# Rotary embedding and score matrices: which five loads GpSimd issues, and where their leftover rows go

## The chip, the core and the metric

The kernel runs on one core of a Trainium2 chip. The core has a matrix engine (TensorE, PE in the profile), three engines for elementwise work (VectorE or DVE, ScalarE or ACT, GpSimd or POOL), a queue engine (SyncE or SP) and sixteen DMA engines that move data between HBM and the on-chip memory SBUF. The metric is the device time of one execution in microseconds (us); lower is better.

## The reference: what is computed

For 16 batches, 512 positions, 16 heads and 64 dimensions, q and k are rotated by tables of cosines and sines, and then, for each position, every head of q is multiplied with the heads of k at all positions of the same batch and head:

```python
q1, q2 = q[..., :half_dim], q[..., half_dim:]
q_rot = np.concatenate([
    q1 * cos_q - q2 * sin_q,
    q1 * sin_q + q2 * cos_q
], axis=-1)
# k_rot in the same way
scores = np.einsum('bshd,bthd->bsht', q_rot, k_rot)
```

All is float32. The inputs q and k are 33.6 MB each, the output (16, 512, 16, 512) is 268.4 MB, so the kernel writes four times what it reads.

## The kernel before, in words

A batch is cut into four tiles of 128 positions (position p*4+c goes to partition p of tile c), so there are 64 tiles in all. Per tile, VectorE rotates q and k in place with three instructions of 128x1024 each (`rope`: two products, lines 153 and 154, and one sum, line 158). PE transposes the rotated rows against an identity matrix, four 128x128 blocks into a PSUM bank (`transposed`, line 174), and VectorE (q) or ScalarE (k, from batch 2 on) copies a bank to SBUF (line 189). PE then computes the scores of one tile, two heads at a time, in eight steps (`scores`, line 205), ScalarE copies each 128x1024 result into a staging buffer (line 212), and after the eighth step the buffer, 4 MB, is stored (line 192). There are three staging buffers.

The first batch is handled in small pieces: its q and k come in several early loads, and its output leaves in sixteen stores of 1 MB (line 215). From batch 1 on, a tile's turn in the main loop contains the eight score steps, the transposes of the next tile of q (at steps 1 and 3) and of the tile of k four ahead (steps 5 and 6), and the rotation of q two tiles ahead and of k five tiles ahead. The order of instructions on every engine is the written order.

The inputs of batches 1 to 15 are loaded whole: `load(which, b)` reads 2 MB, 128 rows of 16 KB. There are two buffers for q and two for k. In the main loop, `load("q", b+2)` stands behind the third tile of batch b and `load("k", b+3)` behind the fourth. Most loads are one DMA on SP's queue (line 126), the same queue that carries all stores. Such a DMA is cut over the sixteen DMA engines, eight rows for each. Stores are cut in the same way (eight rows of 32 KB for each engine).

Five loads go another way, through `load_around`. GpSimd issues them on its own DMA queue, q0 in the profile, where a DMA of n rows with n up to 15 takes n engines one after the other, starting at a cursor that stands behind the last engine used. The main part of the load is the first 120 rows: they go to fifteen engines, eight rows each, in two pieces of 8 KB per row. The cursor is placed so that these fifteen are all but engine 4 (`SLOW = 4`: the DMA starts at engine 5). The cursor is placed by tiny DMAs (`move_cursor`, line 87): n rows of a few bytes into a scratch tile move it by n. The remaining eight rows, 120 to 127, are the leftover. For the loads of k, GpSimd issues them as eight pieces of 2 KB per row with the cursor at 8, one row per engine on engines 8 to 15. For the loads of q, ScalarE's DMA queue (q10) issues them, eight rows on the eight lowest engines, 0 to 7, engine 4 among them. All of these pieces are issued on line 102.

The names that matter below: `RELIEVED` says which loads go this way and in which order (the value counts them, and the first one, 0, resets the cursor); `pieces(queue, lo, hi, F)` issues rows lo to hi in parts of F elements.

Of the kernel before, what the change touches and what calls it, by code (L numbers as in the profile page):

```python
# [10 lines left out]
def kernel(  # L11
# [8 lines left out]
    nc = tc.nc  # L20
# [4 lines left out]
    B, S, H, D = q.shape  # L25
    HD = D // 2
    P = 128
    C = S // P
# [45 lines left out]
    batches = {}  # L74

    RELIEVED = {("q", 6): 0, ("k", 7): 1, ("q", 11): 2, ("k", 12): 3, ("q", 15): 4}
    SLOW = 4
    scratch = const_pool.tile([P, 96], fp32, name="scratch")
    tiny = [0]  # L80

    def move_cursor(n):

        y = tiny[0]
        tiny[0] += 1
        src = bass.AP(q.tensor, 512 * y, [(512, n), (64, 2), (1, 2)])
        nc.gpsimd.dma_start(scratch[:n, 4 * y : 4 * y + 4].rearrange("p (a b) -> p a b", a=2), src)

    def load_around(which, b, t):

        n, E, SMALL = 120, C * H * D, C * H * D // 8
        x = RELIEVED[which, b]
        d = dram[which][b]

        def pieces(queue, lo, hi, F):
            k = E // F
            src = bass.AP(d.tensor, d.offset + lo * E + E - F, [(E, hi - lo), (-F, k), (1, F)])
            v = t[lo:hi].rearrange("p c e -> p (c e)")  # L100
            dst = bass.AP(v.tensor, v.offset + E - F, [v.ap[0], (-F, k), (1, F)])
            queue.dma_start(dst, src)  # L102

        if x == 0:
            nc.gpsimd.inc_swdge_sem([], [], mode="reset_dge_cursor")
        else:

            move_cursor(16 - SLOW)
        if x % 2:
            move_cursor(8)  # L110
            pieces(nc.gpsimd, n, P, SMALL)
        move_cursor(SLOW + 1)
        pieces(nc.gpsimd, 0, n, E // 2)
        if not x % 2:
            pieces(nc.scalar, n, P, SMALL)

    def load(which, b):

        if b >= B:
            return  # L120
        t = in_pool.tile([P, C, H * D], fp32, tag=which + "_in", name=which + "_sb")
        batches[which, b] = t
        if (which, b) in RELIEVED:
            load_around(which, b, t)
        else:
            nc.sync.dma_start(t.rearrange("p c (h d) -> p c h d", h=H), dram[which][b])
# [199 lines left out]
```

## Time and profile before

| what | us |
|---|---|
| median of three runs | 792.46 (792.38 to 793.31) |
| the profiled execution, its span from the first to the last instruction | 789.9 |
| PE busy | 687.7 (87%) |
| ACT busy | 561.2 (71%) |
| DVE busy | 543.8 (69%) |
| POOL busy | 11.9 (2%) |

The profile gives the profiled execution's time as its span; the 2.5 us between it and the median lie outside of the span (start and end of a launch). The page's slices cut the span into 40 equal parts; the digit of the DMA row is the mean busy share of the sixteen DMA engines in tenths, 9 standing for 90% or more. DMA queues are listed with packets, megabytes and their share of the time of sixteen engines: q1 is SP's queue, q0 GpSimd's, q10 ScalarE's, and q8 and q14 fetch instructions. A row of waits reads: who waited, for whom, microseconds in total, how many times, and the longest. A row of DMA issues gives the tile, the queue, how often, the size of each and the median time from issue to landing.

The HBM traffic is 67.24 MB read and 268.44 MB written, 425 GB/s over the span.

### The profile page before, as it was taken

How to read it: one execution, taken by the hardware profiler on the slowest of the kernel's cores; microseconds unless marked ns; L12 is line 12 of the kernel's file. 1: busy time of each engine (PE TensorE's matmuls, PEld its weight loads, DVE VectorE, ACT ScalarE, POOL GpSimd, SP SyncE). 2: the span in 40 equal slices, each digit the busy share in tenths (PEclk: the TensorE clock that was granted, in tenths of full speed). 3: DMA queues.
4: the chain of work that ended last, by engine and by line, in shares of the span. 5: the costliest groups of instructions: out<-in, count | busy, mean ns of one | idle time of the engine just before them, and what ended most of it. 6: DMA issues, size and time to landing. Idle time of an engine off the chain costs nothing.

```text
span 789.9 us, 7753 instructions
## 1 busy us (share of the span) xinstructions
PE 687.7 (87%) x3072; PEld 297.4 (38%) x3072; DVE 543.8 (69%) x516; ACT 561.2 (71%) x647; POOL 11.9 (2%) x24
## 2 busy tenths in 40 slices
PE   4999998989978989798897988989899798899960
PEld 2444443433423434243343433434334343344420
DVE  7999987667855859566676666767678486587400
ACT  3888886866847868486685865877577586588770
POOL 0000000000001000000000000100000000000000
PEclk9999999999998999899899898999899899899995
DMA  9999999999999999999999999999999999999997
GB/s 353 421 426 440 429 431 435 424 434 440 428 427 429 429 425 406 428 431 436 430 431 434 427 431 427 429 432 429 427 437 422 437 433 433 428 431 436 430 431 339
DMA packets 19100, 336.18 MB, mean 426 GB/s; under 512 B 2376, under 2 KB 3656, under 8 KB 4936
## 3 DMA queue, kind: packets, MB, share of 16 engines
q1 hardware_dynamic: 16288, 324.61, 96.1%
q0 software_dynamic: 1872, 10.10, 3.1%
q10 hardware_dynamic: 904, 0.98, 0.4%
q8 instruction: 24, 0.39, 0.2%
q14 instruction: 12, 0.10, 0.0%
HBM read 67.24 MB, written 268.44 MB: 425 GB/s over the span
## 4 chain that ended last, share of the span: by engine, by line
DMA 46%; PE 39%; DVE 7%; ACT 4%; issue 1%; ACTq 0%
DMA out_dram<-st 45%; PE ps L205 29%; PE bank L174 9%; ACT st L212 4%; DVE part L153 2%; DVE early L154 1%; DVE early L158 1%; DMA early<-in_q_dram 1%; DVE k_sb L158 1%; DVE k_sb L154 1%; DVE kT_t L189 0%; DVE q_sb L154 0%; DVE q_sb L158 0%; ACTq L321 0%; DVE qT_t L189 0%
## 5 line engine op out<-in xcount | busy, mean ns | idle before, releaser
L212 ACT COPY st<-ps 128x1024 f32<-128x1024 f32 x512 | 495.0, 1020 | 193.7 <-DMA out_dram<-st 109.1
L205 PE MATMUL ps<-kT_t,qT_t 64*128 64x512 f32 x2048 | 545.6, 650 | 64.3 <-ACT st L212 64.1
L205 PEld LDWEIGHTS ps<-kT_t,qT_t 64*128 64x128 f32 x2048 | 183.3, 196 | 255.3 <-issue 135.4
L189 DVE COPY qT_t<-bank 128x512 f32<-128x512 f32 x118 | 81.5, 690 | 186.5 <-PE bank L174 186.5
L174 PEld LDWEIGHTS bank<-ident,q_sb 128*128 128x128 f32 x480 | 55.4, 151 | 100.5 <-issue 97.6
L174 PE MATMUL bank<-ident,q_sb 128*128 128x128 f32 x480 | 86.8, 308 | 0.4 <-PE ps L205 0.4
L174 PEld LDWEIGHTS bank<-ident,k_sb 128*128 128x128 f32 x480 | 50.3, 140 | 94.6 <-issue 42.3
L174 PE MATMUL bank<-ident,k_sb 128*128 128x128 f32 x480 | 78.6, 287 | 1.2 <-DVE qT_t L189 1.2
L153 DVE TENSOR_TENSOR part<-k_sb,ss_t 128x1024 f32<-128x1024 f32 x60 | 72.9, 1215 | 9.3 <-DMA k_sb<-in_k_dram 9.2
L189 ACT COPY kT_t<-bank 128x512 f32<-128x512 f32 x122 | 72.4, 598 | 6.9 <-PE bank L174 6.9
L154 DVE TENSOR_TENSOR k_sb<-k_sb,cos_t 128x1024 f32<-128x1024 f32 x60 | 73.5, 1225 | 2.0
L158 DVE TENSOR_TENSOR k_sb<-k_sb,part 128x1024 f32<-128x1024 f32 x60 | 73.5, 1225 | 2.1
L154 DVE TENSOR_TENSOR q_sb<-q_sb,cos_t 128x1024 f32<-128x1024 f32 x60 | 73.5, 1225 | 2.1
L153 DVE TENSOR_TENSOR part<-q_sb,ss_t 128x1024 f32<-128x1024 f32 x60 | 73.5, 1224 | 2.0
L158 DVE TENSOR_TENSOR q_sb<-q_sb,part 128x1024 f32<-128x1024 f32 x60 | 72.9, 1215 | 0.0
L174 PE MATMUL bank<-ident,early 128*128 128x128 f32 x64 | 10.5, 316 | 12.2 <-DVE early L158 9.7
L174 PEld LDWEIGHTS bank<-ident,early 128*128 128x128 f32 x64 | 8.3, 161 | 17.3 <-issue 13.9
L153 DVE TENSOR_TENSOR part<-early,ss_t 128x1024 f32<-128x1024 f32 x8 | 9.8, 1222 | 5.7 <-DMA early<-in_k_dram 4.9
L102 POOL DMA_DIRECT2D q_sb<-in_q_dram x3 | 2.3, 754 | 617.4 <-PE bank L174 617.4
L158 DVE TENSOR_TENSOR early<-early,part 128x512 f32<-128x512 f32 x16 | 10.3, 685 | 0.2
L154 DVE TENSOR_TENSOR early<-early,cos_t 128x1024 f32<-128x1024 f32 x8 | 9.8, 1225 | 0.3
L189 ACT COPY qT_t<-bank 128x512 f32<-128x512 f32 x10 | 5.7, 628 | 3.3 <-PE bank L174 3.3
(12 smaller groups left out, 15.9 us busy)
## 6 DMA issues: line engine op xcount, KB each, us to landing
out_dram<-st SPq DMA_DIRECT2D x60, 4096.0 KB, 25.2
k_sb<-in_k_dram SPq DMA_DIRECT2D x13, 2048.0 KB, 27.7
q_sb<-in_q_dram SPq DMA_DIRECT2D x12, 2048.0 KB, 27.6
out_dram<-st SPq DMA_DIRECT2D x16, 1024.0 KB, 14.5
q_sb<-in_q_dram POOLq DMA_DIRECT2D x3, 1920.0 KB, 29.2
k_sb<-in_k_dram POOLq DMA_DIRECT2D x2, 1920.0 KB, 43.2
early<-in_k_dram SPq DMA_DIRECT2D x1, 1536.0 KB
early<-in_q_dram SPq DMA_DIRECT2D x1, 1536.0 KB, 12.4
```

What stands on the lines that cost most here:

```text
L102: queue.dma_start(dst, src)
L153: nc.vector.tensor_tensor(pv, xs, ss, op=mult)
L154: nc.vector.tensor_tensor(xc, xc, cs, op=mult)
L158: nc.vector.tensor_tensor(y, y, z, op=add)
L174: nc.tensor.transpose(bank[:, x, :], src, ident)
L189: copy(out=dst, in_=src)
L205: nc.tensor.matmul(out=po, lhsT=lhs[64 * r : 64 * r + 64, :], rhs=rh, start=True, stop=True)
L212: nc.scalar.copy(out=so, in_=si)
```

## The change

The five loads that GpSimd issues are now all of q: batches 5, 8, 11, 13 and 15. Before, they were q of batch 6, k of 7, q of 11, k of 12 and q of 15. The main part is the same: rows 0 to 119 on all engines but 4.

The leftover rows now go to four engines, 14, 15, 0 and 1 (`AHEAD = 14`: the first of the four), always on GpSimd's queue: the cursor is moved to 14, rows 120 to 123 are issued (one row per engine, two parts of 8 KB), the cursor is moved by 12 and so is back at 14, rows 124 to 127 are issued in the same way, the cursor is moved by 3 to engine 5, and then come the 120 rows. So each of the four engines moves two leftover rows per load, 32 KB, and ScalarE issues no part of a load any more. In the first of the five the cursor starts from a reset (move by 14), in the others from engine 4, where the 120 rows leave it (move by 10).

```diff
-    RELIEVED = {("q", 6): 0, ("k", 7): 1, ("q", 11): 2, ("k", 12): 3, ("q", 15): 4}
-    SLOW = 4
+    RELIEVED = {("q", 5): 0, ("q", 8): 1, ("q", 11): 2, ("q", 13): 3, ("q", 15): 4}
+    SLOW, AHEAD = 4, 14
...
-        n, E, SMALL = 120, C * H * D, C * H * D // 8
+        n, E = 120, C * H * D
...
         if x == 0:
             nc.gpsimd.inc_swdge_sem([], [], mode="reset_dge_cursor")
-        else:
-
-            move_cursor(16 - SLOW)
-        if x % 2:
-            move_cursor(8)
-            pieces(nc.gpsimd, n, P, SMALL)
-        move_cursor(SLOW + 1)
+        move_cursor(AHEAD if x == 0 else (AHEAD - SLOW) % 16)
+        pieces(nc.gpsimd, n, n + 4, E // 2)
+        move_cursor(12)
+        pieces(nc.gpsimd, n + 4, P, E // 2)
+        move_cursor((SLOW + 1 - AHEAD - 4) % 16)
         pieces(nc.gpsimd, 0, n, E // 2)
-        if not x % 2:
-            pieces(nc.scalar, n, P, SMALL)
```

## The prediction

> **What bounds the kernel now.** I read the page's slices first, then its chain, then the queues, then the transfers in narrow windows at the end of the span.
>
> ```profile
> span 789.9 us, 7753 instructions
> DMA  9999999999999999999999999999999999999997
> DMA 46%; PE 39%; DVE 7%; ACT 4%; issue 1%; ACTq 0%
> q1 hardware_dynamic: 16288, 324.61, 96.1%
> q0 software_dynamic: 1872, 10.10, 3.1%
> q10 hardware_dynamic: 904, 0.98, 0.4%
> q8 instruction: 24, 0.39, 0.2%
> q14 instruction: 12, 0.10, 0.0%
> ```
>
> The DMA engines are full in every slice but the last, and the five queues add up to 99.8% of sixteen engines. The chain names PE for 39%, but PE waits there for stage buffers, and so for stores. The bytes do not change here, so a gain can come only from how they are spread over the sixteen engines. The last microseconds show how uneven they are now (windows 781 to 783.5, to 786.5, to 787.5 and to 790 us; each engine's last packet is the 4-byte semaphore write of the last store, so "under 512 B" counts the engines that finish):
>
> ```profile
> DMA packets 33, 0.95 MB, mean 380 GB/s; under 512 B 4, under 2 KB 4, under 8 KB 4
> ...
> DMA packets 30, 0.88 MB, mean 295 GB/s; under 512 B 3, under 2 KB 3, under 8 KB 3
> ...
> DMA packets 9, 0.16 MB, mean 164 GB/s; under 512 B 4, under 2 KB 4, under 8 KB 4
> ...
> DMA packets 5, 0.00 MB, mean 0 GB/s; under 512 B 5, under 2 KB 5, under 8 KB 5
> ```
>
> Four engines are done 5 to 6 us before the last five. To say which, I followed the packet records from end to start: on one engine a packet starts 3 to 4 ns before the recorded end of the one before it, and the order of sizes on each queue is known, so the records fall into sixteen chains from 15 us on, with no idle gap over 0.5 us. The trace names no engine; the split loads do. Eight chains move the small k pieces that GpSimd issues (engines 8 to 15 by the cursor), eight the small q pieces of ScalarE's queue (0 to 7), and one of these eight never gets a data packet of the 120-row loads (4). Ends of the last store:
>
> - upper eight: 782.35, 782.53, 786.35, 786.67, 787.87, 788.25, 788.55, 788.62
> - lower eight: 783.22, 783.32, 785.43, 785.89, 787.05, 787.32, 787.34, 788.52; engine 4 is 787.34 or 788.52, since its chain can't be told from another's for a while
>
> The mean is 786.2. The 24 fetches of q8 (16 KB, 0.88 to 1.05 us each, and the store packet beside one some 0.4 us longer) go round eight chains: the six late upper ones and two lower ones, three each. Those of q14 fall on lower chains. The four early chains carry no fetch. Engine 4 is slow in another way: its 32 KB store packets take about 1246 ns in most stages against 1213 on the others, and 1500 beside a 120-row load.
>
> **The change, part by part.** Durations are those of the profiled execution. Its span is 789.9; the median of the runs is 792.46, so I add 2.5 for what lies outside the span.
>
> *Leftover rows onto four engines.* In each of five loads eight 16 KB rows go to engines 14, 15, 0 and 1: two rows, four 8 KB packets each. 20 packets at 309 ns (every 8 KB packet of q0 on nearly every chain) are 6.18 us per receiver; the worst chain mean, 315 ns, would make 6.3. I take 6.18.
>
> *Old leftover pieces gone.* An upper engine loses eight 4 KB packets (26.23 of q0 time less 25.04 on a chain without them: 1.19 us). A lower one loses 24 pieces of 2 KB and their semaphores on q10: 2.04 us. ScalarE loses three DMA issues (0.72 to 1.29 us); it is 71% busy and ends no wait here, so nothing. If that cover failed it would be under 3 us spread over three stages.
>
> *Engine 4.* It keeps five skipped loads and loses its 2.04 us of q pieces. Its excess over 1213 ns near the two relieved pairs and the last load is about 6, 5 and 0.6 us by the chains; alone the q loads cost 0.6 to 2 each, the k loads 3.3 to 4.3. Five q loads make 3 to 10 instead of some 11.5. Between "one microsecond more" and "eight less" I take 2 to 6 less: it ends well before the others and decides nothing.
>
> *Cursor moves and empty turns.* 30 DMAs on q0 instead of 18: twelve more semaphore packets, four more cursor moves, and on engines that get no piece two placeholders per piece (before, four per k piece on the lower eight). About 35 tiny packets at 7 to 9 ns are 0.3 us per engine. Upper bound: the 290 ns that a turn costs engine 4 beside a 120-row load, 20 turns, 5.8 us; lower bound nothing. I take 0.3, since the lower engines' empty turns at 262 to 267 us are followed by 1213 ns store packets as usual.
>
> *GpSimd's queue and the landing of q.* All five loads now have two pieces and two cursor moves ahead of the 120 rows.
>
> ```profile
> DVE part L153 <- DMA k_sb<-in_k_dram: 9.2, 2, 4.6
> POOL q_sb L102 <- PE bank L174: 617.4, 3, 225.4
> q_sb<-in_q_dram POOLq DMA_DIRECT2D x3, 1920.0 KB, 29.2
> k_sb<-in_k_dram POOLq DMA_DIRECT2D x2, 1920.0 KB, 43.2
> ACT st L212 <- DMA out_dram<-st: 109.1, 41, 6.2
> ```
>
> A q load with nothing ahead lands in 29.2 us, a k load behind pieces in 43.2, and VectorE waited 4.6 us for each such k. On an engine q0 and q1 take turns, one packet each, so what stands ahead costs turns: 2+1, 1+1, 2+1, 1+1, ten turns at 1.22 us, and four more issues on GpSimd, 2.3 us. So q lands 42 to 44 us after the first issue (with a k load of SP's queue in between, whose packets take 0.61 us, some 4 us less). It is needed, by the first product on it, 40.9, 41.3 and 41.3 us after GpSimd's issue for batches 6, 11 and 15. So VectorE waits 0 to 3 us at up to five places. Behind it stand the qT copy of the next tile, then PE's transposes into that bank, four groups later. The cover is the stores already queued: mid-kernel each is issued 6 to 15 us before the fastest engine is done with the one before; the least is 3.2 us (issue at 731.09, first landing of the previous store 734.31). The k waits of 4.6 left no gap in any chain, so these cost nothing; without the cover it is at most 3 us, and only the last load, at 709, comes where stages are as short as 10.02 us. The k waits go, and were hidden too. SP loses the q loads of batches 5, 8, 13 and gets k 7, k 12 and q 6; GpSimd starts a q load some 6.5 us before SP would (227.75 against a store at 234.23), which moves no byte off an engine.
>
> *Sum, by engine:*
> - receivers, upper: 782.5 + 6.18 - 1.19 + 0.3 = 787.8; lower: 783.3 + 6.18 - 2.04 + 0.3 = 787.7
> - upper six with fetches: 788.62 - 1.19 + 0.3 = 787.7 at the latest
> - other lower ones: 788.52 - 2.04 + 0.3 = 786.8 at the latest
>
> The last end moves from 788.6 to 787.8: 0.8 us earlier, a span of 789.1, a time of 791.7 (-0.1%).
>
> **Rivals.**
>
> *Better balance* (0.25). Perfect balance would end all at the mean, 786.2 and 0.3 more: 2.1 us less, 790.4. What could bring it there: at 299 to 308 us, just behind the first pair, load packets on all chains take up to 1765 ns instead of 611, about 1 us per engine, and again weakly at 545 to 553. If the pairs cause that, it goes: 0.8 + 1.0, 790.7. Against it: nothing in the records ties the two.
>
> *A receiver is not an early engine* (0.12, the other side). The trace shows that two upper and two lower engines are early, not that they are 14, 15, 0 and 1. For it speaks that the fetches run through two lower and six upper chains in a fixed cycle, which fits 6 to 13 in a row; a falling order would fit too and make 8 and 9 the early ones. Then a late upper engine gets the rows: 788.6 + 6.18 - 1.19 + 0.3 = 793.9, 5.3 us more, 797.7. It costs over 0.2% as soon as one receiver ends after 784.9 now. Against a slow engine 15: no upper chain has a mean store packet above 1217 ns. The Trainium skill (DMA: Bandwidth & Descriptors, Latency and other measured facts) says that engines 7 and 15 are usually slower in traces, which would speak against giving 15 more; the trace disagrees, its slow engine is among the lower eight and skips the 120-row loads, so I give that rule no more than a part of this chance. By it the sum would be near this rival's, by the trace it stays as above.
>
> *Late q in the last stages* (0.06). If batch 15 lands like the k rows, waiting 4.6 us and 2.3 for the issues, less the 3.2 of margin: 3.7 us lost of the gain, 795.4. It decides from a wait of 3.2 us on.
>
> *The cursor misses* (0.03). Moves of 14, 10, 4 and 3 rows are not in this trace (5, 8, 12 and 120 are). If one did not advance by one engine per row, engine 4 would get five loads back, 80 packets of 309 ns: some 24 us more, about 815.
>
> **Numbers.** Forecast, with nearby outcomes inside 0.2%: 0.54. That 0.2% (1.6 us) is about what a measurement of this kernel can tell from no change. Faster 0.25 is the first rival; slower 0.21 is the other three. The range reaches from perfect balance (790.3) to a loss of 1.2 us (793.7: tiny packets at a quarter of their upper bound, or a late batch 15); it leaves out the wrong receivers, the cursor and the worst of the late q, some 0.18. The likeliest case's own range is 790.9 to 792.6.
>
> **What would show it.** Last store: engines finishing from about 784 to 787.8, none between 781 and 783.5. Queue q0 up by 0.1 to 0.2 points of its share and q10 down by 0.1. VectorE waiting for q_sb up to 3 us, k_sb waits gone, slices still full. It is wrong if four engines finish several us after the rest, if DMA slices fall below 9, or if engine 4's store packets stay above 1500 ns for long.

## The result, and the profile after

The changed kernel takes 797.12 us (796.24 to 797.77) against 792.88 for the kernel before beside it: 1.0051 times as long, 95% interval 1.0040 to 1.0063, 4.2 us slower. The forecast was 791.7. The profiled execution has a span of 795.4 and a time of 797.33, so 1.9 us lie outside the span. (It is 1.8 to 2.0 in the executions of both kernels measured since; the prediction's 2.5 was this and a profiled execution before that was some 0.6 to 0.7 faster than its median.)

The page of the changed kernel: span, slices, the chain, and the queues with packets, megabytes and share.

```profile
span 795.4 us, 7765 instructions
DMA  9999999999999999999999999999999999999996
DMA 49%; PE 37%; DVE 5%; ACT 5%; issue 1%; ACTq 0%; DVEq 0%
q1 hardware_dynamic: 16288, 324.61, 95.5%
q0 software_dynamic: 2320, 10.49, 3.4%
q10 hardware_dynamic: 688, 0.59, 0.2%
q8 instruction: 24, 0.39, 0.2%
q14 instruction: 13, 0.10, 0.0%
```

The slices are still full and the bytes of the queues are what the change says (0.39 MB moved from q10 to q0), yet the span is 5.5 longer. Nothing waits for a late q or k: among the waits that a DMA ends, those of VectorE are for the first batch alone, and ScalarE's for a free staging buffer is what it was (109.1 before). The 120 rows land 37.8 us after their issue (last line).

```profile
ACT st L208 <- DMA out_dram<-st: 110.6, 36, 6.7
...
DVE part L149 <- DMA early<-in_k_dram: 4.9, 1, 4.9
...
q_sb<-in_q_dram POOLq DMA_DIRECT2D x5, 1920.0 KB, 37.8
```

So the loss must lie in how the sixteen engines end. These are the windows 785 to 790, to 792, to 793.5 and to 796 of the changed kernel; "under 512 B" counts engines that finish.

```profile
DMA packets 46, 1.08 MB, mean 216 GB/s; under 512 B 13, under 2 KB 13, under 8 KB 13
...
DMA packets 5, 0.10 MB, mean 49 GB/s; under 512 B 2, under 2 KB 2, under 8 KB 2
...
DMA packets 1, 0.03 MB, mean 22 GB/s; under 512 B 0, under 2 KB 0, under 8 KB 0
...
DMA packets 1, 0.00 MB, mean 0 GB/s; under 512 B 1, under 2 KB 1, under 8 KB 1
```

From 792 on one engine works alone, for two more microseconds. The packet records, followed into sixteen chains as before, say which: the receivers are the four chains with 100 packets of 8 KB on q0. They end at 793.97, 791.48, 790.68 and 788.32; the other twelve at 786.2 to 789.4. The last receiver carries three fetches of q8 (16 KB each), the second six of q14; the other two carry none. So two of the four receivers are not early engines.

The mean over the sixteen chains rose as well, from 786.2 to 788.5. By class, for one engine: 8 KB packets and leftovers 24.9 us before, 26.5 after; SP's load packets 0.3 more; tiny packets 0.25 more. The 8 KB packets take 310 to 470 ns instead of 309 on most of the twelve others near the loads of batches 13 and 15, where the store queue almost ran empty: a store is issued at 595.76, and the first landing of the previous one is at 595.86. On one chain it did run empty, four times between 695 and 737 us, for 0.2 to 0.9 us each. The margin was 3.2 us at the least before. It went as the landings of one store spread over 12 us (6 to 8.5 before): a staging buffer comes free only when the slowest engine is done with it. Why an 8 KB packet then takes longer is not shown.

### The profile page after: what moved, and what is told of

It reads as the page before. It is cut to its first block, busy times and chain, and to the rows that moved or that the text cites. A ratio compares the mean times of both kernels' runs of the same rounds, so it can differ in the third digit from the quotient of the medians.

```text
span 795.4 us, 7765 instructions
## 1 busy us (share of the span) xinstructions
PE 684.2 (86%) x3072; PEld 295.2 (37%) x3072; DVE 544.5 (68%) x516; ACT 561.7 (71%) x647; POOL 19.0 (2%) x36
## 4 chain that ended last, share of the span: by engine, by line
DMA 49%; PE 37%; DVE 5%; ACT 5%; issue 1%; ACTq 0%; DVEq 0%
DMA out_dram<-st 48%; PE ps L201 28%; PE bank L170 9%; ACT st L208 5%; DVE part L149 2%; DVE early L154 1%; DVE k_sb L150 1%; DVE k_sb L154 1%; DVE early L150 1%; DVE kT_t L185 0%; DMA early<-in_k_dram 0%; DVE q_sb L150 0%; DVE q_sb L154 0%; ACTq L317 0%; DVE qT_t L185 0%
## 5 line engine op out<-in xcount | busy, mean ns | idle before, releaser
L201 PE MATMUL ps<-kT_t,qT_t 64*128 64x512 f32 x2048 | 543.8, 648 | 73.3 <-ACT st L208 73.1
L170 PE MATMUL bank<-ident,q_sb 128*128 128x128 f32 x480 | 85.0, 303 | 0.9 <-PE ps L201 0.9
L102 POOL DMA_DIRECT2D q_sb<-in_q_dram x15 | 9.8, 652 | 653.0 <-PE bank L170 509.1
L87 POOL DMA_DIRECT2D scratch<-in_q_dram x15 | 8.7, 581 | 0.4 <-issue 0.4
## 6 DMA issues: line engine op xcount, KB each, us to landing
q_sb<-in_q_dram POOLq DMA_DIRECT2D x5, 1920.0 KB, 37.8
```

Of the source, the lines that this page charges most:

```text
L170: nc.tensor.transpose(bank[:, x, :], src, ident)
L201: nc.tensor.matmul(out=po, lhsT=lhs[64 * r : 64 * r + 64, :], rhs=rh, start=True, stop=True)
```

## The experiments

Two theories at first. R: the loss is placement, two rows per load on engines that are not early. S: it is what every engine pays (the other loads, ten more turns ahead of the 120 rows, more cursor moves, later q). All times are medians, beside the kernel before on the same chip; ratios have 95% intervals.

| run | time | ratio | interval |
|---|---|---|---|
| the change | 797.12 | 1.0051 | 1.0040 to 1.0063 |
| new loads, old leftovers | 792.56 | 1.0003 | 0.9994 to 1.0012 |
| old loads, new leftovers | 798.41 | 1.0073 | 1.0057 to 1.0090 |
| receivers 15, 0, 1, 2 | 795.24 | 1.0035 | 1.0022 to 1.0048 |
| receivers 11, 12, 13, 14 | 797.04 | 1.0057 | 1.0043 to 1.0072 |
| receivers 15, 0, 7, 8 | 806.26 | 1.0176 | 1.0159 to 1.0193 |
| eight receivers, two pieces (30 DMAs) | 795.19 | 1.0033 | 1.0020 to 1.0046 |
| the same, 8 more moves (38) | 795.13 | 1.0037 | 1.0023 to 1.0050 |
| eight receivers, one piece (20 DMAs) | 793.09 | 1.0000 | 0.9992 to 1.0009 |
| the same, piece cut in two (25) | 793.91 | 1.0017 | 1.0007 to 1.0026 |
| one piece, 10 more moves (30) | 793.53 | 1.0013 | 1.0005 to 1.0022 |
| before, scratch 32 columns wider | 795.29 | 1.0041 | 1.0028 to 1.0053 |
| before, scratch 128 columns wider | 792.77 | 1.0002 | 0.9993 to 1.0011 |

Four more runs are given in the text: the two with markers, and two with more moves in a wider scratch tile.

### The two halves of the change

The new choice of loads with the old way for the leftover rows:

```diff
-    RELIEVED = {("q", 6): 0, ("k", 7): 1, ("q", 11): 2, ("k", 12): 3, ("q", 15): 4}
+    RELIEVED = {("q", 5): 0, ("q", 8): 1, ("q", 11): 2, ("q", 13): 3, ("q", 15): 4}
```

> One part of the change alone: the five loads are q of batches 5, 8, 11, 13 and 15, but the leftover rows go where they went before (ScalarE's queue for three loads, GpSimd on engines 8 to 15 for two). Theory R (two of the four receivers were not early engines; the last engine is a receiver that also carries fetches of q8): no receiver is overloaded, so 791.5 to 793.5, within 0.2% of before, and the last engine ends 5 us earlier than in the changed kernel. Rival S (the choice of loads costs: five q loads, late ones above all, let the queue of stores run dry on the fast engines): 795 to 798, most of the loss stays.

And the other half, the changed kernel with the loads of before:

```diff
-    RELIEVED = {("q", 5): 0, ("q", 8): 1, ("q", 11): 2, ("q", 13): 3, ("q", 15): 4}
+    RELIEVED = {("q", 6): 0, ("k", 7): 1, ("q", 11): 2, ("k", 12): 3, ("q", 15): 4}
```

> The other part alone: the loads of before (q 6, k 7, q 11, k 12, q 15), but the leftover rows on engines 14, 15, 0 and 1. R: the same 160 KB on the same four engines, so 796 to 798, some 0.5% slower than before, one engine 2 us or more behind all others in the last store. S: 792 to 794, at most a third of the loss, since the pairs and not five q loads set the pace of the stores.

The first took 792.56, no change; the second 798.41. So the choice of loads costs nothing, and the leftover rows carry the whole loss. Windows 785 to 790, to 793, to 794.5 and to 797 of the second show the same two stragglers (one of the 14 is the last packet of the store before, at 785.84):

```profile
DMA packets 49, 1.15 MB, mean 229 GB/s; under 512 B 14, under 2 KB 14, under 8 KB 14
...
DMA packets 6, 0.16 MB, mean 55 GB/s; under 512 B 1, under 2 KB 1, under 8 KB 1
...
DMA packets 2, 0.03 MB, mean 22 GB/s; under 512 B 1, under 2 KB 1, under 8 KB 1
DMA packets 1, 0.00 MB, mean 0 GB/s; under 512 B 1, under 2 KB 1, under 8 KB 1
```

By the chains they are again the receiver with three q8 fetches (795.2) and the one with six q14 (793.5). The second half is 1.3 us slower than the whole change (the intervals overlap); in it a k load with pieces ahead comes late, and VectorE waits for it:

```profile
DVE part L149 <- DMA k_sb<-in_k_dram: 36.6, 3, 19.8
```

### Which engines carry the fetches

Marker DMAs with packets of sizes that nothing else has, so that a chain shows its engine. First sixteen of two rows in the changed kernel, then fifteen of three rows in the kernel before, behind each of two loads (each moves the cursor by 3, so each engine gets two or three of the sizes). The small tile that takes the markers is not shown:

```diff
+    def mark(first):
+        for j in range(first, first + 8):
+            w = 20 + j
+            src = bass.AP(q.tensor, 4096 * j, [(512, 2), (1, w)])
+            nc.gpsimd.dma_start(marks[2 * j : 2 * j + 2, :w], src)
...
+        if x == 0:
+            mark(0)
+            move_cursor(3)
+            mark(8)
```

> The changed kernel with sixteen tiny DMAs of two rows each, of sixteen different sizes, behind the first split load: each lands on two neighbouring engines by the cursor, so that a chain of packets can be named by the two sizes that it holds. It costs some 34 tiny packets, 0.3 us per engine, and 797 to 798. R: of engines 14, 15, 0 and 1 one of the first two carries three fetches of q8 and ends last, one of the last two carries six of q14, and two carry none; two early engines are among 2 to 13. S: the names do not matter; the last engine need not be a receiver.

```diff
+        if x in (0, 2):
+            for j in range(15):
+                w = 10 + j
+                src = bass.AP(q.tensor, 4096 * j, [(512, 3), (64, 2), (1, w)])
+                nc.gpsimd.dma_start(marks[3 * j : 3 * j + 3, : 2 * w].rearrange("p (a b) -> p a b", a=2), src)
```

> The kernel before with fifteen tiny DMAs of three rows each (two runs of a size of its own per row) behind the split loads of q 6 and of q 11. Each takes three neighbouring engines and moves the cursor by three, three times round the sixteen with another offset each time, so that the three sizes on a chain of packets give its engine. Some 60 tiny packets, 0.5 us per engine: 792 to 795. R: the eight chains that fetch for q8 include just one of the engines 14 and 15; of 0 and 1 one carries the six fetches of q14; the early engines are one of 14 and 15, one of 0 and 1, and at least two others between 2 and 13. If 14, 15, 0 and 1 turn out to be the four early ones, R falls.

The first told little: all sixteen markers fell on the same two chains, both of them receivers, so a plain two-row DMA did not follow the cursor (800.19 in one execution). The second took 829.97, far from what was expected of it: its markers stood ahead of the pieces of k, and VectorE waited for k. (Part of both times is probably not the markers' doing: their tile, 160 and 192 bytes per partition, shifts the tiles behind it, and 16 KB load packets take some 700 and 684 ns in the mean between 70 and 80 us, against 611 in the kernel before. The last experiments are about that.)

```profile
DVE part L160 <- DMA k_sb<-in_k_dram: 76.5, 2, 38.6
```

But it names the engines. The q8 fetches go round engines 11, 12, 13, 14, 5, 6, 9, 10, three each. Those of q14 fall on engine 1 (six), 3 (most of the others) and 4. Free of fetches are 0, 2, 7, 8 and 15. Two lower and six upper engines, as the prediction had found, but not 6 to 13: of the receivers, 14 carries three q8 fetches and 1 carries six of q14.

### The receivers moved by one, moved by three, and onto free engines

```diff
-    SLOW, AHEAD = 4, 14
+    SLOW, AHEAD = 4, 15
```

> The changed kernel with the four receivers shifted by one engine: 15, 0, 1 and 2 instead of 14, 15, 0 and 1. Nothing else differs. R: engine 14 (three fetches of q8, last at 794.0 us) is relieved of 6.2 us, and engine 1 (six fetches of q14, 791.5) becomes the last: 2 to 3 us less than the changed kernel, 794 to 795.5, still 0.2% slower than before. S: the amount moved and the order are the same, so 796.5 to 798.

```diff
-    SLOW, AHEAD = 4, 14
+    SLOW, AHEAD = 4, 11
```

> Edit: the changed kernel with AHEAD = 11, so the receivers are engines 11, 12, 13 and 14; pieces, moves and bytes are the same. By the map of the fetches all four carry three fetches of q8, and by the chains before they end at 786.3 to 788.6. R: four engines instead of one end late, each at 786.3 to 788.6 - 1.19 + 6.18 + 0.3 = 791.6 to 793.9, the other twelve by 788; the last end is hardly later than in the changed kernel, so the time is 796.5 to 798.5. If the map is wrong and these are free engines, they end near 788 and the time is 792 to 793. S (what all engines pay): 797, but with the ends of the twelve others late too.

With receivers 15, 0, 1 and 2 the time falls by 1.9 us to 795.24, as R said, and the chain that ends last (791.8) is the receiver with q14 fetches, engine 1. By the ratios the gain is 1.3 us, and the two intervals overlap. Windows 788 to 791 and 791 to 793:

```profile
DMA packets 10, 0.16 MB, mean 55 GB/s; under 512 B 5, under 2 KB 5, under 8 KB 5
...
DMA packets 1, 0.00 MB, mean 0 GB/s; under 512 B 1, under 2 KB 1, under 8 KB 1
```

With receivers 11 to 14 R said four late ends instead of one, and a time that hardly moves: 797.04, and windows 784 to 790 and 790 to 796 are these:

```profile
DMA packets 61, 1.57 MB, mean 262 GB/s; under 512 B 13, under 2 KB 13, under 8 KB 13
...
DMA packets 13, 0.29 MB, mean 49 GB/s; under 512 B 4, under 2 KB 4, under 8 KB 4
```

One of the 13 is the last packet of the store before, at 785.65. Four engines finish at 791.5, 792.4, 793.2 and 795.0, each with 100 packets of 8 KB and three q8 fetches, the other twelve by 788.5. This is the clearest test of the map and of the rows' price: 791.6 to 793.9 was worked out. It also shows that one such engine costs nearly as much as four.

Then the leftovers in two-row pieces on engines that the map calls free (the scratch tile, eight columns wider for the moves, is not shown):

```diff
+        move_cursor(15 if x == 0 else 11)
+        for y in range(4):
+            pieces(nc.gpsimd, n + 2 * y, n + 2 * y + 2, E // 2)
+            move_cursor(6 if y < 3 else 12)
```

> The changed kernel with the leftover rows on engines 15, 0, 7 and 8, none of which fetches instructions: four pieces of two rows, alternately on 15 and 0 and on 7 and 8, with a cursor move behind each. The bytes per receiver are the same. R: no receiver ends late, so the last engines are fetching ones that get nothing, at 787 to 788 us of the span, and the time is 791 to 792.5, at or a little under before. But twice as many turns stand ahead of the 120 rows (20 instead of 10), so q lands some 12 us later and VectorE waits some 10 us per load: if that runs the queue of stores dry (S), 795 or more.

R was right on the ends: all sixteen engines finish within 2 us (801.1 to 802.9), and at the first load the four chains that get 18 to 20 packets of 8 KB are chains without a fetch. But twenty turns ahead of the 120 rows made q late, and the queue ran dry behind VectorE: two slices fall to 394 and 339 GB/s, where most have 420 to 435.

```profile
DVE part L148 <- DMA q_sb<-in_q_dram: 57.3, 5, 13.9
```

Of the 14 us, some 3 belong to the scratch tile (widened to 104 columns here). That is an estimate from the last experiments; this width was not run alone.

### One row per engine, and what a DMA costs

The same pieces, moves and bytes, on eight engines (15, 0, 1, 2 and 5, 6, 7, 8):

```diff
-        move_cursor(AHEAD if x == 0 else (AHEAD - SLOW) % 16)
+        move_cursor(15 if x == 0 else 11)
         pieces(nc.gpsimd, n, n + 4, E // 2)
-        move_cursor(12)
+        move_cursor(2)
         pieces(nc.gpsimd, n + 4, P, E // 2)
-        move_cursor((SLOW + 1 - AHEAD - 4) % 16)
+        move_cursor(12)
```

> Edit: the changed kernel with the same five loads, the same number of pieces, of cursor moves and of bytes, but rows 120 to 123 go to engines 15, 0, 1, 2 and rows 124 to 127 to engines 5, 6, 7, 8, so that each of eight engines gets one leftover row per load (3.09 us in all) instead of four engines getting two. R (the loss is two rows per load on engines that are not early): no engine gets more than its old small pieces took from it and about 1 us besides; engine 14 ends near 787.5, engines 5 and 6 at 787.3 - 2.04 + 3.09 + 0.3 = 788.7, engine 1 near 788.5; the last store ends 788.6 to 789.6, time 792.0 to 793.5, no difference from the kernel before that can be measured. S (the loss comes from what all engines pay: ten more turns ahead of the 120 rows, more cursor moves, later q, more packets): unchanged from the changed kernel, 796 to 798, whatever engines the rows are on.

795.19: neither theory. Two chains end at 791.5 and 791.8, engines 5 and 6 (90 packets of 8 KB and three q8 fetches), 3 us later than R had them. So placement is not all, and I priced what all engines pay. Empty moves in the loads-only kernel, 30 of them (the scratch tile, 192 columns wide for them, is not shown):

```diff
+        for y in range(6):
+            move_cursor(8)
```

> Edit: the kernel of the loads-only run (the new five loads, the old small leftover pieces) with six more tiny cursor moves of eight rows ahead of each of the five loads: 30 more DMAs on GpSimd's queue, the cursor ends where it was, no leftover row changes its engine. This is the cost that every engine pays in the changed kernel, and more of it (the change adds 12 DMAs), without the placement of the rows. R (placement decides): 792.2 to 793.5, as in the loads-only run, with the 120-row loads landing some 8 to 14 us later and the last store ending within 1 us of that run's. S (late q, turns or packets cost what is left of the loss in the run with eight receivers): 794.5 or more, and VectorE's part waits for q_sb, or the slices drop.

It took 797.06 (1.0065, 1.0048 to 1.0082), which spoke for S. So I varied the number of DMAs around the run with eight receivers: one piece instead of two, and two more moves (these in a scratch tile of 128 columns, not shown).

```diff
-        pieces(nc.gpsimd, n, n + 4, E // 2)
-        move_cursor(2)
-        pieces(nc.gpsimd, n + 4, P, E // 2)
-        move_cursor(12)
+        pieces(nc.gpsimd, n, P, E // 2)
+        move_cursor(14)
```

> Edit: the run with eight receivers, but rows 120 to 127 in one piece on the eight engines 15, 0, 1, 2, 3, 4, 5, 6: four DMAs per load instead of six on GpSimd's queue (20 in all; the kernel before has 18). Engines 5 and 6, the fetch carriers among its receivers, get one row per load as before, and engine 4 gets five rows (3.09 us, and its 290 ns per turn beside them). The run of empty turns cost 4.5 us for 30 DMAs, its chains ended 2.5 us later in the mean, so 0.08 to 0.15 us per DMA. T (what is left of the loss with eight receivers is the DMAs and turns that every engine pays): 0.8 to 1.5 us under that run, 793.7 to 794.4, the 120 rows landing about 5 us earlier. P (it is the row on engines 5 and 6, placement alone): 795, unchanged. If engine 4 has no room for its five rows, it is the last and the time is 795 or more, which the chains tell apart from P.

```diff
         move_cursor(12)
+        move_cursor(8)
+        move_cursor(8)
```

> Edit: the run with eight receivers and two more cursor moves of eight rows between the second piece and the last move of each load: eight DMAs per load instead of six, ten more in all, at the place where the change has its own; every row stays on its engine. T (DMAs and turns cost all engines): 0.8 to 1.5 us more than with six, 796.0 to 796.7, the 120 rows landing some 5 us later. P (placement alone): 794.6 to 795.8, unchanged, unless the later q makes VectorE's part wait for q_sb long enough that GB/s falls in a slice.

793.09 with 20 DMAs (under both answers), 795.19 with 30, 797.82 with 40 (1.0063, 1.0050 to 1.0076): a straight line, and still not to be trusted. The kernels with more moves need a wider scratch tile, and their SP load packets were longer long before GpSimd's queue does anything. Between 70 and 80 us a 16 KB packet takes 611 ns in the mean in the kernel before and in the changed one, 676 with the two more moves, 674 with the empty ones. (The median is 611 in all of them: one packet in five or six takes longer, up to 1782 ns.) So the tile alone:

```diff
-    scratch = const_pool.tile([P, 96], fp32, name="scratch")
+    scratch = const_pool.tile([P, 128], fp32, name="scratch")
```

> Edit: the kernel before with a scratch tile of 128 instead of 96 columns, nothing else: no DMA, no move, no row changes, only the addresses of the tiles behind it shift by 128 bytes per partition. A (the address makes SP's 16 KB load packets longer): load packets longer at 73, 107 and 156 us as in the runs with a wider tile (0.5, 0.2 and 0.2 us per engine there, nothing with 96 columns), time 794.5 to 796.5. N (the width is harmless): 792 to 793.5, no longer packets there.

and the moves alone, in the tile as it was:

```diff
-        move_cursor(12)
+        for n_ in ([12, 8, 8] if x < 4 else [12]):
+            move_cursor(n_)
```

> Edit: the run with eight receivers and two more cursor moves of eight rows in the first four loads (eight DMAs more in all), with the scratch tile of 96 columns as in all kernels but the widened ones. T (every extra DMA of GpSimd's queue costs all engines 0.2 us and more, as between one piece and two): 796.5 to 797.5. A (what the run with two more moves lost came from the wider tile): 794.6 to 796, as with six DMAs per load, and no longer load packets at 73 us.

The tile alone costs 795.29 against 792.04. Window 70 to 80, the kernel before:

```profile
DMA packets 363, 4.60 MB, mean 460 GB/s; under 512 B 44, under 2 KB 44, under 8 KB 44
```

and with the wider tile:

```profile
DMA packets 358, 4.23 MB, mean 423 GB/s; under 512 B 45, under 2 KB 45, under 8 KB 45
```

The eight more moves alone cost nothing (795.13, as with 30 DMAs), although the 120 rows now land 39.8 us after their issue and VectorE waits for them:

```profile
DVE part L150 <- DMA q_sb<-in_q_dram: 13.0, 4, 3.9
```

So the straight line was two things in one, and the runs with empty turns and with two more moves say little on what a DMA costs. The tile's width was then shifted by 512 bytes instead of 128:

```diff
-    scratch = const_pool.tile([P, 96], fp32, name="scratch")
+    scratch = const_pool.tile([P, 224], fp32, name="scratch")
```

> Edit: the kernel before with a scratch tile of 224 instead of 96 columns, nothing else: every tile behind it begins 512 bytes per partition later, at a multiple of 512 again (the input tiles at 19968 instead of 19456). If it is the alignment to 512 bytes that the wider tiles broke (L): 792 to 793.3, and the 16 KB load packets at 72 us take 611 to 615 ns as with 96 columns. If any shift, or losing a multiple of 1024 bytes, is enough (A): 794.5 to 796 and 670 ns or more there.

792.77, no change, and 612.5 ns in the mean:

```profile
DMA packets 357, 4.55 MB, mean 455 GB/s; under 512 B 43, under 2 KB 43, under 8 KB 43
```

So it is an alignment that counts, and not the shift. All tiles behind the scratch tile move together; that the input tiles matter is read from the load packets. No shift by 256 bytes was run, so the boundary may be 256 bytes as well as 512.

What stays of the 2.1 us between one piece and two was split with two runs that keep every row on the engine of the one-piece run:

```diff
-        pieces(nc.gpsimd, n, P, E // 2)
+        pieces(nc.gpsimd, n, n + 4, E // 2)
+        pieces(nc.gpsimd, n + 4, P, E // 2)
```

> Edit: the one-piece run with its piece cut in two, rows 120 to 123 and 124 to 127, one behind the other without a move between, so that every row stays on the engine it has in the one-piece run (15, 0, 1, 2 and 3, 4, 5, 6): five DMAs per load. If two pieces cost what one does not (Q: the second piece's turns), 794.5 to 795.5; if it is where the second piece goes or the cursor's moves (M), 792.3 to 793.6.

```diff
-        move_cursor(14)
+        for n_ in (8, 8, 14):
+            move_cursor(n_)
```

> Edit: the one-piece run with two more cursor moves of eight rows behind the piece, six DMAs per load as in the changed kernel, the 120 rows landing some 4 us later. If DMAs ahead of the 120 rows cost all engines (T), 794.5 to 795.5; if not (the placement decides), 792.3 to 793.6, as with four DMAs.

793.91 lies between the two answers, 793.53 at the upper end of the second. Cutting the piece costs 1.7 parts in a thousand (1.3 us), ten more moves 1.3 (1.0 us). Both lie just outside the interval of the one-piece run, but the intervals overlap. The 120 rows land 33.6 us after their issue with one piece, 36.8 with the moves:

```profile
q_sb<-in_q_dram POOLq DMA_DIRECT2D x5, 1920.0 KB, 36.8
```

So ten DMAs ahead of the 120 rows cost about 1 us here, and eight beyond 30 no more that can be measured. Some of that 1 us may be engine 4's alone, which gets five leftover rows in these three kernels and none in the change. Its chain ends at 786.7 with one piece, at 791.5 with the piece cut (the last of all, in the slowest of that kernel's executions) and at 790.2 with the moves (the last is at 790.25). The one-piece kernel (1.0000) and the one with the new loads alone (1.0003) are the best of the changed kernels, and no faster than the kernel before. Windows 781 to 786.5, to 789 and to 791 of the one-piece kernel; the engine that ends alone, at 789.8, is a receiver with three q8 fetches:

```profile
DMA packets 61, 1.67 MB, mean 304 GB/s; under 512 B 10, under 2 KB 10, under 8 KB 10
...
DMA packets 7, 0.07 MB, mean 26 GB/s; under 512 B 5, under 2 KB 5, under 8 KB 5
DMA packets 1, 0.00 MB, mean 0 GB/s; under 512 B 1, under 2 KB 1, under 8 KB 1
```

## Why the prediction was wrong

- **What bounds the kernel** held: the bytes are the same, the slices full, and the last engine's end sets the time.
- **The step that failed is the sum by engine**, where the receivers were given the chains that end at 782.5 and 783.3. That 14, 15, 0 and 1 are those chains rested on one guess, that the fetches run over 6 to 13 in a row. They run over 11 to 14, 5, 6, 9 and 10, and q14's over 1, 3 and 4. For 15 and 0 the sum gave 787.8 and 787.7; the two receivers without fetches ended at 790.7 and 788.3. Engine 14 is one of the late upper ones. Engine 1 is the lower one with six q14 fetches, which ended at 785.89 before and not at 783.3. The sum also gave every chain 0.3 us more, and the mean over the sixteen rose by 2.3. Of this 1.6 is longer 8 KB packets and pieces; with receivers 15, 0, 1 and 2 they take 25.0 us per engine, as before.
- **The rival "a receiver is not an early engine" is what happened**, with its price: 793.9 worked out, 793.97 measured; 797.7 for the time, 797.12 measured. Its mechanism was right (a late upper engine gets the rows), its example (a falling order, 8 and 9 early) was not, and 0.12 was too little for a guess on which the sign hung. That the price agrees to 0.1 us is partly luck: it takes the latest upper chain (788.6) for engine 14, which may be any of the six that ended from 786.35 on, and the same sum is 0.5 and 2.9 us short for the two receivers without fetches. Moving the receivers by one and by three confirmed it.
- **The terms** of 6.18 for the rows and 1.19 for the pieces that go held but for one engine: four carriers came to 791.5, 792.4, 793.2 and 795.0 where 791.6 to 793.9 follows from them. That ScalarE "ends no wait here" was too strong, since PE waits 64.1 us for it in all before; with its three issues gone that wait is 73.1 us, so no gain shows.
- **Cursor moves and empty turns**, taken at 0.3 from bounds of 0 and 5.8, look mis-sized. Their own packets do take 0.25 us more per engine, but ten more DMAs cost about 1.0 us by the run that adds them alone (the change adds twelve), with the reservations made there. With 1.2 instead of 0.3 the forecast would have been 792.6, still inside its range.
- **GpSimd's queue and the landing of q** held on balance: the k waits are gone, q landed 37.8 us after the issue of the 120 rows, and where it came late enough to hold VectorE (up to 3.9 us with eight more moves) it cost nothing that could be measured. The cover that was named shrank, though, from 3.2 us to 0.1 at 595.76, and to nothing on one chain. Where that cover is gone, with twenty turns ahead of the rows, waits of up to 13.9 us reach the DMA queue.
- **Engine 4** decides nothing in the change, as said, but no relief by 2 to 6 us shows at its end. The chain that is slow in its way can't be followed without doubt, and ends at 786.8 or 788.7 (787.3 or 788.5 before); with the new loads and the old leftovers it ends at 789.2.
- **The other rivals**: the cursor did not miss (each receiver has its 20 packets more), better balance did not come. The long load packets behind the first pair did go, as that rival hoped: between 295 and 310 us 16 KB packets took 1.1 us per engine beyond 611 ns each before, and 0.03 in the changed kernel. But as many came behind other loads, 2.0 us per engine over the span against 1.7. Of the rule that speaks against 15 (the Trainium skill, DMA: Bandwidth & Descriptors, Latency and other measured facts: engines 7 and 15 are usually slower in traces) no run here shows anything. With receivers 15, 0, 1 and 2 the last chain is the one with q14 fetches, and where 7 and 15 each got a row per load the two late ones were the carriers 5 and 6.

The 4.2 us are then, by estimate: 1.3 to 1.9 for engine 14 (the change against receivers 15, 0, 1, 2, by ratios and by medians), about 1.0 for the DMAs at most, and the rest, 1.3 to 1.9, that these runs do not split. Engine 1, which receives two rows in both kernels and ends last when 14 is left out, is a candidate that was not tried alone. Open too is why two pieces with their second on 5, 6, 7 and 8 cost 1.3 to 1.6 us more than the one-piece kernel with a cut or with moves; their intervals overlap.

## What to carry to other kernels

When the DMA engines bound a kernel, the last microseconds of the trace show who ends late, but a chain is not an engine: before work is moved to "the early ones", put markers on them and read their names, away from loads that something waits for. Price what every engine pays (turns, moves) with a run of its own. And when an experiment needs a larger tile, run the larger tile alone: its address may cost more than what is being measured.

## What was not expected of the hardware

- A shift of the input tiles (and of all tiles behind them) by 128 bytes per partition cost 3.3 us (1.0041): 16 KB load packets take 677 ns in the mean instead of 611 between 70 and 80 us. A shift by 512 bytes costs nothing (1.0002, 612.5 ns). Shifts of 32 bytes (684 ns) and 384 bytes (674 ns) made the packets longer as well. Whether a multiple of 256 bytes is enough was not run.
- The instruction fetches of q8 go round a fixed set of eight of the sixteen engines (11, 12, 13, 14, 5, 6, 9, 10), each three times in this kernel. A fetch takes 0.88 to 1.05 us, and in the kernel before four of the engines without any were done by 783.3, all others at 785.4 or later.
- Two-row DMAs of one run of elements per row did not follow the cursor of GpSimd's queue (sixteen in a row went to the same two engines, in one execution); those of two runs per row did, with two, three and four rows.
